# First stage of a two-layer DiT kernel: squares summed by TensorE in four pairs, first projection pair in halves of k, sine chains moved

## The chip, the cores and the metric

The kernel runs on one core of a Trainium2 chip. The metric is the device time of one execution in microseconds; lower is better. The engines are named as in the profile: PE (matmul), PEld (its weight load), DVE (VectorE), ACT (ScalarE), POOL (GpSimd), SP (the engine that issues the DMAs). PE has two clock levels, 1.2 and 2.4 GHz; a granted clock of 0.50 is the lower, 1.00 the upper.

## The reference, cut to what matters

Two layers on 512 latent and 256 context tokens, width 1024. What the change touches is the start of layer 0: the modulation vectors, the first RMS norm, the first columns of the projection `w_in`, and the small sine network that makes the convolution filters.

```python
sh1, sc1, ... = ada_mod(c, ada_w[0], ada_b[0])          # silu(c) @ w + b, in six chunks
csh1, csc1, ... = ada_mod(c_ctx, ada_w[0], ada_b[0])
h_lat = rmsnorm(x_lat, norm_mix[0]) * (1 + sc1) + sh1    # x * rsqrt(mean(x*x) + eps) * gain
h_ctx = rmsnorm(x_ctx, norm_mix[0]) * (1 + csc1) + csh1
u = h @ w_in                                             # x0, x1, v of the hyena half, q, k, v of the mLSTM half
u = dwconv(u[:, :1536], hy_conv_w) + hy_conv_b; g = v * x1
# filters: sin of a linear map, twice, then a linear map times a decay
h = sin(freq * (z @ fw1 + fb1)); h = sin(freq * (h @ fw2 + fb2)); h = (h @ fw3) * (decay + shift)
```

## The kernel before

The two token sets are laid side by side: a tile of x is 128 features x 768 tokens (512 + 256, the list `ALL`), and there are eight of them (k = 0 to 7). A product in f32 is made of three matmuls, high by high, high by low and low by high part, all on line 128 (`gemm`); for one k and one output block these are six matmuls, since each is made once for the 512 tokens and once for the 256. The high part of a weight block (`wh`) is cast by ACT on line 99 and the low part (`wl` = `raw` - `wh`) made by DVE on line 100. A "pair" below is two output blocks of 128 columns, one of v and one of x1 of the hyena half, which are made together.

The work of the stage, in the order of the source (lines 473 to 525): eight squares on ACT (lines 204 and 207) that DVE adds up in seven adds (line 208); six matmuls with a column of ones that sum over the features (line 214); the reciprocal square root on small DVE operations; six matmuls that spread it over 128 partitions (line 225), copied by ACT (line 481). `ada_pe` makes one chunk of the modulation vectors: eight matmuls of raw rows (line 278; a record pair for each), a copy by ACT (line 281), four matmuls with two columns (line 284) and the addition of the bias on DVE (line 93, `mod`). `sin_layer` is called twice: a matmul of 64 rows (line 373), six DVE operations on 64x768 (lines 377 to 382) and the sine on ACT (line 385), the second from the output of the first. Then, for every k: the scaled tile (`t`, line 96, DVE), the high part of h (line 522, ACT), its low part (line 96, DVE), and twelve matmuls of the first pair. `mod` has chunk 0 (shift, first half of k) and chunk 2 (scale, first half) ahead of k = 0, chunks 3 and 1 (the second half) ahead of k = 4. Behind the first pair come the convolution of its output (`conv`, three operations for each of 512 and 256 tokens: one on ACT, line 536, two on DVE, line 96), the filters (line 400, exponentials on line 402, sums and differences on lines 424 to 427) and the second pair.

The framework has a scheduler: the source gives each operation a priority, and the order on each engine is what the scheduler makes of it and of the tiles that are free. PSUM is split into three buffers `m`, two `g` and one `a`; there are five large temporaries `t`, four `u`, and two each of `raw`, `wh` and `wl`. Each engine runs its own queue strictly in that order, so a waiting instruction holds up all that stand behind it on its engine.

Of the kernel before, what the change touches and what calls it, by code (L numbers as in the profile page):

```python
# [12 lines left out]
ALU = mybir.AluOpType  # L13
# [4 lines left out]
P = 128  # L18
# [32 lines left out]
def hybrid_kernel(ctx: ExitStack, tc: tile.TileContext, A, out):  # L51
# [34 lines left out]
    def atile():  # L86
        return pa.tile([P, 512], F32, tag="a", name=nm("a"))
# [122 lines left out]
    def norm_scale(acc, n, dim, mid=None):  # L210
        nt = n // P
        ps = mtile()
        for i in range(nt):
            pe.matmul(ps[:, i:i + 1], acc[:, i * P:(i + 1) * P], ones[:, 0:1], start=True, stop=True)
        ms = sp.tile([P, 6], F32, tag="n1", name=nm("ms"))[:, :nt]
        y = sp.tile([P, 6], F32, tag="n2", name=nm("y"))[:, :nt]
        t = sp.tile([P, 6], F32, tag="n3", name=nm("nt"))[:, :nt]
        dve.tensor_scalar(ms, ps[:, :nt], 1.0 / (dim * RS * RS), EPS / (RS * RS), op0=ALU.mult, op1=ALU.add)
        rsqrt(y, ms, t)
        if mid:  # L220
            mid()
        g = [mtile() for _ in range((nt + 3) // 4)]
        for i in range(nt):
            o = g[i // 4][:, i % 4 * P:(i % 4 + 1) * P]
            pe.matmul(o, y[:, i:i + 1].to_broadcast([P, P]), ident, start=True, stop=True)
        return g
# [46 lines left out]
    def ada_pe(layer, ch):  # L273
# [7 lines left out]
        act.copy(ys, y)  # L281
        ps = atile()
# [87 lines left out]
    def sin_layer(w, kdim, b, rows=1):  # L370
        g = gtile()
        for z, (lo, n) in zip(hs_z, ALL):
            pe.matmul(g[:64, lo:lo + n], w, z[:kdim, :], start=True, stop=True)
        a = temp2()[:64]
        k = temp2()[:64]
        fb, fq = vec(b)[:64, :], vec("hy_freq")[:64, :]
        dve.tensor_scalar(a, g[:64, :T], fb, fq, op0=ALU.add, op1=ALU.mult)
# [97 lines left out]
    acc = temp()  # L475
    for k in range(KD):
        norm_acc(acc, x[k], k == 0)
    gp = norm_scale(acc, T, D)
# [3 lines left out]
    ada_pe(0, 2)  # L482
    w_first = [load_wk(A["w_in"][8], KD)]
# [26 lines left out]
    mod_half(0)  # L510
    for k in range(KD):
        if k == 3:
            ada_pe(0, 3)
            ada_pe(0, 1)
            mod_half(1)
        t = slot(4 + k, [P, 2, T], F32R)
        h.append((t[:, 0, :], t[:, 1, :]))
        f = temp()
        for c, (lo, n) in enumerate(ALL):
            s = slice(lo, lo + n)  # L520
            stt(f[:, s], x[k][:, s], a[:, k, c:c + 1], gsb0[:, s], ALU.mult, ALU.mult)
            act.activation(h[k][0][:, s], f[:, s], AF.Identity, bias=b[:, k, c:c + 1])
            stt(h[k][1][:, s], f[:, s], b[:, k, c:c + 1], f32(h[k][0][:, s]), ALU.add, ALU.subtract)
        for ps, w in ((first_v, w_first[0]), (first_x, w_first[1])):
            gemm(ps, w, h, ALL, ks=[k], first=k == 0, last=k == KD - 1)
    filter_fold()
# [979 lines left out]
```

## Time and profile before

| | us |
|---|---|
| runs shown | 1771.18, 1772.79, 1776.69 |
| median of them | 1772.79 |
| profiled execution | 1769.59 |
| its span, first to last instruction | 1767.8 |
| PE busy in the span | 1687.9 (95%) |
| first product of the first pair starts | 47.77 |
| last product of the first pair ends | about 75.3 |

PE is the engine that sets the end nearly everywhere; the stage that is changed lies in the first 78 us, where it isn't. The mean granted clock of the span is 0.987. In the trace the clock stands at 0.50 until 27.19 us (the records begin there), at 1.00 until 37.43, at 0.50 until 51.08, and then at 1.00 until 221.7. Times in the rows are us from the span's start; a matmul in f32 leaves two records.

### The profile page before, as it was taken

The numbers are of one execution on the slowest core, as the hardware profiler recorded it, in microseconds if no ns is written. First come the engines' busy times: TensorE is split into PE (matmuls) and PEld (weight loads), VectorE is DVE, ScalarE is ACT, GpSimd is POOL, SyncE is SP. The second block draws the span as 40 slices with busy tenths as digits, with TensorE's granted clock in tenths as the row PEclk, the third lists the DMA queues.
The fourth block names the chain that finished last, engine by engine and source line by source line (L and its number), as shares of the span: only waits on it lengthen the run. The fifth ranks groups of instructions, "written<-read, shape, count | busy, mean of one in ns | idle before, by whom it ended". The sixth has DMA issues, their size and how long they took to land.

```text
span 1767.8 us, 24375 instructions
## 1 busy us (share of the span) xinstructions
PE 1687.9 (95%) x9657; PEld 1435.2 (81%) x9657; DVE 1082.8 (61%) x1843; ACT 642.4 (36%) x1089; POOL 162.7 (9%) x165
## 2 busy tenths in 40 slices
PE   3989989998899999999999999989999999999997
PEld 2668777887888888888888888978888888888886
DVE  5786767749967456764355446487884644444445
ACT  3434232346543321132311334455553432232233
POOL 0141233005113000000000000000000300000001
PEclk9999989999999999999999999999999999999998
DMA  9026546412523134543255223110022223323322
GB/s 340 12 85 242 191 149 214 136 66 72 179 84 108 60 108 131 179 156 98 82 166 170 70 63 115 38 34 28 26 100 72 72 96 95 96 95 95 95 85 84
DMA packets 65748, 193.85 MB, mean 110 GB/s; under 512 B 7102, under 2 KB 17152, under 8 KB 65634
## 3 DMA queue, kind: packets, MB, share of 16 engines
q1 hardware_dynamic: 65634, 192.29, 33.4%
q8 instruction: 76, 1.25, 0.3%
q14 instruction: 38, 0.31, 0.1%
HBM read 178.64 MB, written 13.63 MB: 109 GB/s over the span
## 4 chain that ended last, share of the span: by engine, by line
PE 60%; issue 22%; DVE 7%; ACT 2%; POOL 1%; POOLq 0%; DVEq 0%; ACTq 0%
PE g L128 47%; PE g L1245 2%; DVE s L96 1%; DVE t L93 1%; PE m L1263 1%; PE m L104 1%; PE m L105 1%; PE m L103 1%; PE m L128 1%; DVE s L100 1%; PE g L103 1%; PE g L104 1%; PE g L105 1%; PE a L104 1%; PE a L103 1%
## 5 line engine op out<-in xcount | busy, mean ns | idle before, releaser
L128 PE MATMUL g<-s,wh 128*128 128x512 f32 (+1 forms) x4440 | 1067.2, 349 | 3.6 <-ACT u L1254 1.4
L128 PEld LDWEIGHTS g<-s,wh 128*128 128x128 f32 x4440 | 721.5, 189 | 124.6 <-issue 5.2
L128 PE MATMUL g<-s,wl 128*128 128x512 f32 (+2 forms) x2220 | 650.2, 348 | 1.9 <-DVE wl L100 1.9
L99 ACT CAST wh<-raw 128x1024 fp32r<-128x1024 f32 (+4 forms) x217 | 210.9, 972 | 646.5 <-PE g L128 556.4
L128 PEld LDWEIGHTS g<-s,wl 128*128 128x128 f32 x2220 | 365.5, 188 | 59.9 <-DVE wl L100 3.4
L100 DVE TENSOR_TENSOR wl<-raw,wh 128x1024 fp32r<-128x1024 f32 (+4 forms) x217 | 248.0, 1144 | 226.0 <-ACT wh L99 221.2
L96 DVE SCALAR_TENSOR_TENSOR acc<-ada,sc,acc 128x512 f32<-128x512 f32 x224 | 162.6, 763 | 27.7 <-DMA ada<-in_ada_dram 26.1
L96 DVE SCALAR_TENSOR_TENSOR s<-g,mod,s 128x512 f32<-128x512 f32 (+1 forms) x104 | 63.0, 625 | 146.0 <-PE g L128 145.2
L96 DVE SCALAR_TENSOR_TENSOR t<-g,vecs,t 128x511 f32<-128x511 f32 x200 | 128.5, 643 | 27.8 <-ACT t L536 22.8
L93 DVE TENSOR_TENSOR t<-t,g 128x768 f32<-128x768 f32 (+2 forms) x52 | 41.3, 794 | 109.2 <-PE g L128 109.1
L536 ACT ACTIVATE t<-g,vecs 128x512 f32<-128x512 f32 x84 | 58.5, 696 | 87.7 <-DVE t L96 62.4
L1245 PE MATMUL g<-s,s 128*128 128x512 f32 (+1 forms) x320 | 64.7, 344 | 3.7 <-DVE s L93 2.6
L1245 PEld LDWEIGHTS g<-s,s 128*128 128x128 f32 x320 | 48.8, 188 | 10.8 <-DVE s L93 4.1
L1078 ACT ACTIVATE t<-t 128x768 f32<-128x768 f32 (+1 forms) x42 | 31.0, 739 | 68.8 <-DVE t L96 68.8
L250 POOL TENSOR_SCALAR t<-t,A,mod 128x256 f32<-128x256 f32 x20 | 21.5, 1074 | 373.7 <-DVE t L93 364.5
L100 DVE TENSOR_TENSOR s<-m,s 128x512 fp32r<-128x512 f32 (+1 forms) x90 | 50.3, 590 | 6.9 <-ACT s L99 6.6
L99 ACT CAST s<-m 128x512 fp32r<-128x512 f32 (+1 forms) x90 | 42.5, 514 | 32.3 <-PE m L1263 24.2
L207 ACT ACTIVATE t<-s 128x256 f32<-128x256 f32 (+2 forms) x60 | 31.9, 549 | 29.7 <-DVE s L96 24.5
L1345 POOL TENSOR_TENSOR s<-s,t 128x256 f32<-128x256 f32 x8 | 5.5, 725 | 361.9 <-ACT t L1341 361.9
L1254 ACT ACTIVATE u<-g,mx 128x768 f32<-128x768 f32 x32 | 28.9, 905 | 25.0 <-DVE mx L1252 25.0
L1188 POOL MEMSET s<- 64x768 f32 x1 | 0.7, 734 | 398.6 <-PE g L128 398.6
L100 DVE TENSOR_TENSOR s<-t,s 128x768 fp32r<-128x768 f32 (+1 forms) x44 | 36.0, 818 | 0.0
(357 smaller groups left out, 1824.2 us busy)
## 6 DMA issues: line engine op xcount, KB each, us to landing
raw<-in_up_dram SPq DMA_DIRECT2D x88, 512.0 KB, 3.5
ada<-in_ada_dram SPq DMA_DIRECT2D x82, 512.0 KB, 3.5
raw<-in_down_dram SPq DMA_DIRECT2D x32, 512.0 KB, 3.6
raw<-in_w_in_dram SPq DMA_DIRECT2D x24, 512.0 KB, 3.7
raw<-in_w_out_dram SPq DMA_DIRECT2D x16, 512.0 KB, 3.4
s<-in_ada_dram SPq DMA_DIRECT2D x14, 512.0 KB, 10.2
s<-in_xT_dram SPq DMA_DIRECT2D x8, 768.0 KB, 4.9
raw<-in_down_dram SPq DMA_DIRECT2D x16, 384.0 KB, 3.1
```

Of the source, the lines that this page charges most:

```text
L93: return dve.tensor_tensor(o, a, b, op=op)
L96: return dve.scalar_tensor_tensor(o, a, s, b, op0=op0, op1=op1)
L99: act.copy(h, src)
L100: eng.tensor_tensor(l, src, f32(h), op=ALU.subtract)
L103: pe.matmul(o, s[0], m[0], start=start, stop=False)
L104: pe.matmul(o, s[0], m[1], start=False, stop=False)
L105: pe.matmul(o, s[1], m[0], start=False, stop=stop)
L128: pe.matmul(ps[r][:, :n] if type(ps) is list else ps[:, lo:lo + n], w[a][:, k - k0, :], mv[k][b][:, lo:lo + n], start=first and k == ks[0] ...
L207: act.activation(sq, xa, AF.Square)
L536: act.activation(d, s, AF.Identity, scale=w[:, 1:2], bias=bias)
L1078: act.activation(t[:, :n], t[:, :n], AF.Silu, **({} if f else dict(bias=zs)))
L1245: pe.matmul(g[:, lo:lo + w_], s_, m_[:, lo:lo + w_], start=n == 0, stop=n == 4)
```

## The change

- `norm_scale` takes a tuple of partial sums. The squares are added in four pairs (four DVE adds, not seven), PE sums each pair (24 matmuls with the ones column, not 6), and one small DVE reduction adds the four.
- The first sine layer (argument, fold, sine) stands ahead of the norm. The argument's matmul of the second layer stands behind the copies of the norm; its fold and its sine stand behind the last chunk of the first pair.
- `ada_pe` is cut in `ada_rows` (matmuls of rows and the copy) and `ada_cols` (the rest). The rows of chunk 2 are issued while DVE makes the reciprocal root (`mid`).
- The loop over k is cut in `first_scaled`, `first_h` and `first_gemm` and written out; chunk k = 3 of the pair is issued in two halves around the columns of the last modulation chunk.

```diff
+        accs = acc if type(acc) is tuple else (acc,)
+        for c, v in enumerate(accs):
+            for i in range(nt):
+                o = c * nt + i
+                pe.matmul(ps[:, o:o + 1], v[:, i * P:(i + 1) * P], ones[:, 0:1], start=True, stop=True)
...
+        if len(accs) > 1:
+            sums = ms
+            dve.tensor_reduce(ms, ps[:, :len(accs) * nt].rearrange("p (c i) -> p i c", i=nt), axis=AX.X, op=ALU.add)
...
+    def sin_arg(w, kdim, b):
+        a = temp2()[:64]
+        fb, fq = vec(b)[:64, :], vec("hy_freq")[:64, :]
         for z, (lo, n) in zip(hs_z, ALL):
-            pe.matmul(g[:64, lo:lo + n], w, z[:kdim, :], start=True, stop=True)
+            g = mtile()
+            pe.matmul(g[:64, :n], w, z[:kdim, :], start=True, stop=True)
+            dve.tensor_scalar(a[:, lo:lo + n], g[:64, :n], fb, fq, op0=ALU.add, op1=ALU.mult)
+        return a
...
-    acc = temp()
-    for k in range(KD):
-        norm_acc(acc, x[k], k == 0)
-    gp = norm_scale(acc, T, D)
+    sin_1 = sin_arg(hs_w3[:33, 1024:1088], 33, "hy_fb1")
+    sin_fold(sin_1)
+    acc = []
+    for k in range(0, KD, 2):
+        acc.append(temp())
+        norm_acc(acc[-1], x[k], True)
+        norm_acc(acc[-1], x[k + 1], False)
+    acc = tuple(acc)
+    w_first = []
+
+    def mod_rows():
+        w_first.append(ada_rows(2))
+
+    gp = norm_scale(acc, T, D, mod_rows)
...
-    ada_pe(0, 2)
-    w_first = [load_wk(A["w_in"][8], KD)]
+    ada_cols(0, 2, w_first.pop())
+    sin_out(sin_1)
+    sin_2 = sin_arg(hs_w3[:64, 1088:1152], 64, "hy_fb2")
+    w_first.append(load_wk(A["w_in"][8], KD))
...
-    ada_pe(0, 0)
-    sin_layer(hs_w3[:33, 1024:1088], 33, "hy_fb1")
-    sin_layer(hs_w3[:64, 1088:1152], 64, "hy_fb2", 2)
...
+    mod_half(0)
+    for k in range(3):
+        first_scaled(k)
+    ada_cols(0, 0, ada_rows(0))
+    first_h(0)
+    first_gemm(0)
+    first_scaled(3)
+    first_h(1)
+    first_gemm(1)
+    r3 = ada_rows(3)
+    for k in (2, 3):
+        first_h(k)
+    first_gemm(2)
+    ada_cols(0, 3, r3)
+    mod_half(1)
+    r1 = ada_rows(1)
+    first_gemm(3, slice(0, 1))
+    for k in range(4, 7):
+        first_scaled(k)
+    ada_cols(0, 1, r1)
+    first_gemm(3, slice(1, 2))
+    first_h(4)
+    first_gemm(4)
+    first_scaled(7)
+    for k in range(5, KD):
+        first_h(k)
+        first_gemm(k)
+    sin_fold(sin_2)
+    sin_out(sin_2, 2)
```

How the instructions then stand, at three places. First PE at the start of the first pair. `m_352` takes the rows of modulation chunk 3, `g_252` the argument of the second sine layer, `acc_88` and `acc_89` hold the output of the first; `g_289` is the v block of the first pair, `s_292` h of k = 0. Before:

```order
L278 MATMUL m_352<-s_267,s_90 32x512
L278 MATMUL m_352<-s_268,s_90 32x512
L278 MATMUL m_352<-s_269,s_90 32x512
L373 MATMUL g_252<-acc_88,s_90 64x512
L373 MATMUL g_252<-acc_89,s_90 64x256
L128 MATMUL g_289<-s_292,wh_208 128x512
L128 MATMUL g_289<-s_292,wh_208 128x256
```

After; here `m_241` takes the second part of that argument (the first stands four rows ahead of it), `m_294` the rows of chunk 0, `a_229` and `a_305` the columns of chunks 2 and 0, and `g_282` and `s_311` are the block and h:

```order
L385 MATMUL m_241<-acc_89,s_90 64x256
L294 MATMUL a_229<-comb,u_216 128x2 x4
L285 MATMUL m_294<-s_106,s_90 32x512
L285 MATMUL m_294<-s_107,s_90 32x512
L285 MATMUL m_294<-s_106,s_90 32x512
L285 MATMUL m_294<-s_107,s_90 32x512
L285 MATMUL m_294<-s_108,s_90 32x512
L285 MATMUL m_294<-s_109,s_90 32x512
L285 MATMUL m_294<-s_108,s_90 32x512
L285 MATMUL m_294<-s_109,s_90 32x512
L294 MATMUL a_305<-comb,u_303 128x2 x4
L128 MATMUL g_282<-s_311,wh_246 128x512
```

The argument of the second sine layer moved from between the modulation rows and the first product to eleven rows ahead of the first product.

Second DVE behind the first pair. `wl_559` (before) and `wl_579` (after) are the low part of the v block of the second pair; `ada_503`, `ada_504` and `ada_523`, `ada_524` the convolved output of the first pair; `t_`, `u_` with an `m_` behind the arrow are filter halves. Before:

```order
L96 SCALAR_TENSOR_TENSOR t_529<-u_526,m_523 128x512
L96 SCALAR_TENSOR_TENSOR u_538<-u_536,m_532 128x512
L100 TENSOR_TENSOR wl_559<-raw_556,wh_558 128x1024
L96 SCALAR_TENSOR_TENSOR ada_503<-g_289,vecs,ada_503 128x511
L96 SCALAR_TENSOR_TENSOR ada_504<-g_290,vecs,ada_504 128x511
L96 SCALAR_TENSOR_TENSOR ada_503<-g_289,vecs,ada_503 128x511
L96 SCALAR_TENSOR_TENSOR ada_504<-g_290,vecs,ada_504 128x511
L96 SCALAR_TENSOR_TENSOR ada_503<-g_289,vecs,ada_503 128x255
L96 SCALAR_TENSOR_TENSOR u_539<-u_536,m_533 128x512
```

After:

```order
L96 SCALAR_TENSOR_TENSOR ada_523<-g_282,vecs,ada_523 128x255
L96 SCALAR_TENSOR_TENSOR ada_524<-g_283,vecs,ada_524 128x255
L96 SCALAR_TENSOR_TENSOR u_558<-u_556,m_552 128x512
L96 SCALAR_TENSOR_TENSOR u_559<-u_556,m_553 128x512
L439 TENSOR_TENSOR u_562<-t_548,u_558 128x512
L441 TENSOR_TENSOR u_563<-t_549,u_559 128x512
L440 TENSOR_TENSOR t_548<-t_548,u_558 128x512
L442 TENSOR_TENSOR t_549<-t_549,u_559 128x512
L93 TENSOR_TENSOR s_511<-u_562,s_510 128x512
L93 TENSOR_TENSOR s_515<-t_548,s_514 128x512
L93 TENSOR_TENSOR s_517<-u_563,s_516 128x512
L100 TENSOR_TENSOR wl_579<-raw_576,wh_578 128x1024
```

The low part moved from ahead of the convolution to behind the convolution, the filter halves, their sums and differences and three of their low parts.

Third PE at the start of the second pair, whose v block is `m_568`, `m_569` before. Before:

```order
L128 MATMUL g_290<-s_467,wl_219 128x512
L128 MATMUL g_290<-s_467,wl_219 128x256
L400 MATMUL m_533<-s_90,acc_88 128x512
L128 MATMUL m_568<-s_292,wh_558 128x512
L128 MATMUL m_569<-s_292,wh_558 128x256
L128 MATMUL m_568<-s_292,wh_558 128x512
L128 MATMUL m_569<-s_292,wh_558 128x256
L128 MATMUL m_568<-s_292,wl_559 128x512
L128 MATMUL m_569<-s_292,wl_559 128x256
```

After, where it is `m_588`, `m_589`, and `g_590` is its x1 block:

```order
L415 MATMUL m_552<-s_90,acc_88 128x512
L415 MATMUL m_553<-s_90,acc_88 128x512
L128 MATMUL m_588<-s_311,wh_578 128x512 x2
L128 MATMUL g_590<-s_311,wh_584 128x512
L128 MATMUL g_590<-s_311,wh_584 128x256
L128 MATMUL g_590<-s_311,wh_584 128x512
L128 MATMUL g_590<-s_311,wh_584 128x256
L128 MATMUL m_589<-s_311,wh_578 128x256 x2
L415 MATMUL m_706<-s_90,acc_88 128x512
L128 MATMUL m_588<-s_311,wl_579 128x512
L128 MATMUL m_589<-s_311,wl_579 128x256
L128 MATMUL m_588<-s_331,wh_578 128x512
```

The first matmul with the low part, `wl_579`, now has eight matmuls with high parts and five filter matmuls (three of them shown) between it and the first pair; all that use h of k = 1 and later stand behind it.

## Rows read from the trace of the kernel before

**Rows 1.** The page's head: the span, and busy time of each engine.

```profile
span 1767.8 us, 24375 instructions
PE 1687.9 (95%) x9657; PEld 1435.2 (81%) x9657; DVE 1082.8 (61%) x1843; ACT 642.4 (36%) x1089; POOL 162.7 (9%) x165
```

**Rows 2.** Windows: start:end, us, busy of each engine (records), clock, DMA share, GB/s.

```profile
27.20:37.40 10.20, 6.53 (x50) 2.79 (x42) 7.49 (x15) 2.75 (x5) 0.00 (x0) 1.00 1.03 397
47.77:51.10 3.33, 3.33 (x11) 2.85 (x11) 3.15 (x5) 0.00 (x0) 0.00 (x0) 0.50 0.00 0
51.10:66.31 15.21, 14.55 (x85) 9.04 (x83) 6.18 (x14) 7.70 (x13) 0.00 (x0) 1.00 0.00 0
66.31:75.36 9.05, 9.05 (x50) 7.39 (x49) 6.86 (x15) 3.71 (x7) 0.00 (x0) 1.00 0.01 3
```

**Rows 3.** Timeline of PE, first stage: start, us, line, out<-in, count, [idle before <-releaser].

```profile
17.40 2.72 PE L214 MATMUL m<-ones,t 128*128 128x1 f32 x12 [10.31 <-DVE t L208]
...
24.84 3.07 PE L278 MATMUL m<-s,s 128*32 128x512 f32 x16
...
29.64 1.94 PE L278 MATMUL m<-s,s 128*32 128x512 f32 x16
...
45.02 2.82 PE L373 MATMUL g<-acc,s 64*64 64x512 f32 x4 [9.78 <-ACT acc L385]
47.77 1.65 PE L128 MATMUL g<-s,wh 128*128 128x512 f32 x4
...
64.40 1.98 PE L400 MATMUL m<-s,acc 64*128 64x512 f32 x6
66.31 1.53 PE L128 MATMUL g<-s,wh 128*128 128x512 f32 x5
```

**Rows 4.** Timeline of ACT and POOL: sines, table load, last squares, filter fold.

```profile
13.93 1.58 ACT L207 ACTIVATE t<-s 128x768 f32<-128x768 f32 x2 [0.41 <-DMA s<-in_xT_dram]
44.34 0.94 ACT L385 ACTIVATE acc<-u 64x512 f32<-64x512 f32 x2 [2.47 <-DVE u L382]
61.87 1.28 ACT L402 ACT_TABLE_LOAD   x1
```

```profile
40.00 3.56 POOL L390 TENSOR_TENSOR s<-s 64x512 f32<-64x512 f32 x2 [39.55 <-DMA s<-in_fw_dram]
```

**Rows 5.** Timeline of DVE, first stage and the hand-over to the second pair.

```profile
15.33 2.01 DVE L208 TENSOR_TENSOR t<-t,t 128x768 f32<-128x768 f32 x2
...
32.02 3.65 DVE L96 SCALAR_TENSOR_TENSOR t<-s,A,t 128x256 f32<-128x256 f32 x7
35.59 1.06 DVE L377 TENSOR_SCALAR u<-g,vecs 64x768 f32<-64x768 f32 x1
36.58 0.15 DVE L93 TENSOR_TENSOR mod<-a,vecs 128x8 f32<-128x8 f32 x1
...
42.36 1.48 DVE L96 SCALAR_TENSOR_TENSOR s<-t,mod,s 128x256 fp32r<-128x256 f32 x1
...
75.08 1.22 DVE L100 TENSOR_TENSOR wl<-raw,wh 128x1024 fp32r<-128x1024 f32 x1 [2.19 <-ACT wh L99]
```

**Rows 6.** Timeline of PE at the hand-over.

```profile
75.30 1.12 PE L400 MATMUL m<-s,acc 64*128 64x512 f32 x2
76.35 0.97 PE L128 MATMUL m<-s,wh 128*128 128x512 f32 x4
77.16 0.51 PE L128 MATMUL m<-s,wl 128*128 128x512 f32 x2
```

**Rows 7.** Groups of DVE instructions, 66 to 92 us: xcount, busy us, mean ns, idle before.

```profile
L96 DVE SCALAR_TENSOR_TENSOR ada<-g,vecs,ada 128x511 f32<-128x511 f32 x4 | 2.7, 740 | 0.0
L96 DVE SCALAR_TENSOR_TENSOR ada<-g,vecs,ada 128x255 f32<-128x255 f32 x4 | 1.8, 479 | 0.0
L96 DVE SCALAR_TENSOR_TENSOR t<-u,m 128x512 f32<-128x512 f32 x3 | 2.0, 670 | 0.0
L424 DVE TENSOR_TENSOR u<-t,u 128x512 f32<-128x512 f32 x1 | 0.7, 683 | 0.0
L93 DVE TENSOR_TENSOR s<-u,s 128x512 fp32r<-128x512 f32 x2 | 1.4, 690 | 0.0
```

More of the change, by code (lines that the diff above doesn't have):

```diff
@@ L212, in norm_scale @@
         ps = mtile()
-        for i in range(nt):
-            pe.matmul(ps[:, i:i + 1], acc[:, i * P:(i + 1) * P], ones[:, 0:1], start=True, stop=True)
+        accs = acc if type(acc) is tuple else (acc,)
[3 more added lines that the diff above has]
+                pe.matmul(ps[:, o:o + 1], v[:, i * P:(i + 1) * P], ones[:, 0:1], start=True, stop=True)
         ms = sp.tile([P, 6], F32, tag="n1", name=nm("ms"))[:, :nt]
@@ L217, in norm_scale @@
         t = sp.tile([P, 6], F32, tag="n3", name=nm("nt"))[:, :nt]
-        dve.tensor_scalar(ms, ps[:, :nt], 1.0 / (dim * RS * RS), EPS / (RS * RS), op0=ALU.mult, op1=ALU.add)
+        sums = ps[:, :nt]
+        if len(accs) > 1:
+            sums = ms
+            dve.tensor_reduce(ms, ps[:, :len(accs) * nt].rearrange("p (c i) -> p i c", i=nt), axis=AX.X, op=ALU.add)
+        dve.tensor_scalar(ms, sums, 1.0 / (dim * RS * RS), EPS / (RS * RS), op0=ALU.mult, op1=ALU.add)
         rsqrt(y, ms, t)
@@ L271, in hybrid_kernel, with ada_rows @@
     dve.tensor_reduce(comb, ident.rearrange("p (u c) -> p c u", c=32)[:, 0:2, :], axis=AX.X, op=ALU.add)
-    def ada_pe(layer, ch):
+    def ada_rows(ch):
         y = mtile()
@@ L281, in ada_pe, with ada_cols @@
         act.copy(ys, y)
+        return ys
+    def ada_cols(layer, ch, ys):
         ps = atile()
@@ L368, in hybrid_kernel, with sin_fold @@
     kd = dp.tile([6, P, 1536], F32, name="kd")
-    def sin_layer(w, kdim, b, rows=1):
-        g = gtile()
+    def sin_arg(w, kdim, b):
+        a = temp2()[:64]
+        fb, fq = vec(b)[:64, :], vec("hy_freq")[:64, :]
         for z, (lo, n) in zip(hs_z, ALL):
-            pe.matmul(g[:64, lo:lo + n], w, z[:kdim, :], start=True, stop=True)
-        a = temp2()[:64]
+            g = mtile()
+            pe.matmul(g[:64, :n], w, z[:kdim, :], start=True, stop=True)
+            dve.tensor_scalar(a[:, lo:lo + n], g[:64, :n], fb, fq, op0=ALU.add, op1=ALU.mult)
+        return a
+    def sin_fold(a):
         k = temp2()[:64]
-        fb, fq = vec(b)[:64, :], vec("hy_freq")[:64, :]
-        dve.tensor_scalar(a, g[:64, :T], fb, fq, op0=ALU.add, op1=ALU.mult)
         dve.tensor_scalar(k, a, 1.0 / (2.0 * math.pi), MAGIC, op0=ALU.mult, op1=ALU.add)
@@ L382, in sin_layer, with sin_out @@
         dve.tensor_scalar(a, a, 3.1415925, -3.1415925, op0=ALU.min, op1=ALU.max)
+    def sin_out(a, rows=1):
         for z, (lo, n) in zip(hs_z, ALL):
@@ L509, in hybrid_kernel, with first_scaled, first_h, first_gemm @@
     first_v, first_x = gtile(), gtile()
[L510 to L515, printed above, removed]
+    fs = {}
+    def first_scaled(k):
+        fs[k] = temp()
+        for c, (lo, n) in enumerate(ALL):
+            s = slice(lo, lo + n)
+            stt(fs[k][:, s], x[k][:, s], a[:, k, c:c + 1], gsb0[:, s], ALU.mult, ALU.mult)
+    def first_h(k):
+        f = fs.pop(k)
         t = slot(4 + k, [P, 2, T], F32R)
         h.append((t[:, 0, :], t[:, 1, :]))
-        f = temp()
         for c, (lo, n) in enumerate(ALL):
             s = slice(lo, lo + n)
-            stt(f[:, s], x[k][:, s], a[:, k, c:c + 1], gsb0[:, s], ALU.mult, ALU.mult)
             act.activation(h[k][0][:, s], f[:, s], AF.Identity, bias=b[:, k, c:c + 1])
             stt(h[k][1][:, s], f[:, s], b[:, k, c:c + 1], f32(h[k][0][:, s]), ALU.add, ALU.subtract)
-        for ps, w in ((first_v, w_first[0]), (first_x, w_first[1])):
+    def first_gemm(k, part=slice(0, 2)):
+        for ps, w in ((first_v, w_first[0]), (first_x, w_first[1]))[part]:
             gemm(ps, w, h, ALL, ks=[k], first=k == 0, last=k == KD - 1)
+    mod_half(0)
[27 more added lines that the diff above has]
+    sin_out(sin_2, 2)
     filter_fold()
```

## The prediction

> **What bounds the kernel now.** I read the page's head first: PE is busy for 1687.9 of 1767.8 us [rows 1], so over the kernel time is PE's work, and only a stretch in which PE waits, or runs at the lower clock, can give something back. Then the windows and PE's timeline of the first 78 us. The longest wait of PE inside the stage stands ahead of the second sine argument: 9.78 us idle, ended by ACT's sine at 45.02; the argument itself takes 2.82 more, and the first product starts at 47.77 [rows 3]. It starts at the lower clock, which stays until about 51.1 [rows 2]. From 66.31 on PE is busy without a gap (9.05 of 9.05 [rows 2]) to the end of the first pair, which I put at 75.36. So what the stage is worth is where that end falls. Last I read who hands over to the second pair, since a gain counts only if PE can go on: before, PE does one filter matmul and four high-part matmuls and then finds the low part `wl` just made (75.08 + 1.22 = 76.30; the first matmul with it at 77.16 [rows 5, 6]). The hand-over costs 77.16 - 75.36 = 1.8 us, part of it useful work.
>
> **The change part by part: the first stage.** *Sums.* DVE drops three adds, but the last add waits for the last squares as before: they end at 13.93 + 1.58 = 15.5 [rows 4], the last add at 15.33 + 2.01 = 17.34 [rows 5]. The order puts the first sine (0.94 for two [rows 4]) ahead of the last pair's squares on ACT, so that add can come up to 0.9 later; the first three sums lie beside the loading of x, and the last six matmuls cost the 2.72 that all sums cost before [rows 3]. Plus a reduction like the small ones (0.15 to 0.17 [rows 5]): between -1 and +1 us for the norm's end; I take 0, since DVE's queue behind it, below, is what sets the first product.
>
> *Modulation rows and scaled tiles.* Rows 2 move into the wait for the reciprocal root, rows 0 follow. Chunk 0's shift was finished on DVE at 36.58, behind seven scaled tiles (3.65) and the sine's 1.06 at 35.59 [rows 5]. The scaled tiles still stand ahead of it, the 1.06 does not: 36.58 - 1.06 = 35.5, then 0.17 and one 512 wide ACT operation, which I put at 0.7 (a 768 wide square takes 1.58/2 = 0.8 [rows 4]): first product T0 = 36.4 if the clock is raised in time, 11.4 us earlier than 47.77. If PE is still at the lower clock through both groups of rows, each costs 3.07 instead of 1.94 [rows 3], 1.1 more, twice, and the sine argument that now stands ahead of the columns costs up to its 2.82, of which 1.8 remains after overlap by my estimate: T0 = 36.4 + 2.2 + 1.8 = 40.4.
>
> *From the first product to chunk k = 4.* Before this took 66.31 - 47.77 = 18.5 us. PE's work in it, in us at full clock, is 3.33/2 + 14.55 - 1.98 (filter matmuls that now stand behind the pair) = 14.2 [rows 2, 3]; all at the lower clock it is 28.4. Before, the sine wait had let DVE make nearly all scaled tiles and low parts of k = 0 to 3 ahead; now PE starts beside them, and POOL's fold of the filter weights (3.56 us at 40.00 [rows 4]) lies under it, under which a 256 wide low part took 1.48 [rows 5] where its like takes about 0.5. So I take neither end but 22.5 us, 4 more than before, between 14.2 and 28.4. The rest of the pair is k = 4 to 7 and stays 9.05 [rows 2]. End of the pair E: 36.4 + 22.5 + 9.05 = 68.0 with the early clock, 40.4 + 31.55 = 72.0 with the late one. Gain of the stage g = 75.36 - E: 7.4 or 3.4.
>
> *Second sine.* It costs ACT and DVE what it did, and two more table loads at 1.28 each [rows 4]; they lie in ACT's idle time behind the last h, and PE needs the sine for the filters only. I cost it at nothing, because the hand-over below is later; without that cover it would be 1.28.
>
> **The change part by part: the hand-over.** This is the term that decides. In the order of before `wl` of the second pair stands on DVE ahead of the convolution; after, it stands behind all of this, which can begin only at E, because the convolution reads the finished pair and the filters need the matmuls that stand behind the pair on PE: about 1.0 for the first filter matmul (two records 1.12 [rows 6]); four 511 wide operations, 2.7; four 255 wide, 1.8; four filter halves at 0.67, 2.7; four sums and differences at 0.68, 2.7; three low parts at 0.69, 2.1; `wl`, 1.2 [rows 5, 7]. That is 14.2; the rows run into each other by some 0.08 each (four 0.74 in a row took less than their sum), 15 times, 1.2: 13.0 us from E to `wl`. PE has the filter matmuls and eight high-part matmuls to do and then stands; everything of k = 1 and later is queued behind the first `wl` matmul, and since PE runs without gaps from there, the whole rest of the program waits with it. Against that: the 1.8 that the hand-over cost before; and 1.6 of work that PE does in the wait and needn't do later (one filter matmul 0.9, four x1 high-part matmuls 0.7 [rows 6]). And PE idles for about 10 us, as long as the 9.78 us after which the clock stayed low from 45.02 to 51.1 [rows 2, 3], which cost 6.1/2 = 3.0; bounds 0 and 3.0, I take 2.4, because part of the wait is filled with matmuls.
>
> The hand-over loses 13.0 - 1.8 - 1.6 + 2.4 = 12.0 us. **Sum:** 12.0 - g: +4.6 with the early clock, +8.6 with the late one. The stage breaks even only if the pair ends 12.0 us earlier, at 63.4. I see nothing later that gives the loss back: the order is the same there apart from names.
>
> **The base.** The profiled execution took 1769.59, 1.8 outside its span, and is 3.2 below the median, 1772.79. I take the mean of 1769.59, 1771.18 and 1772.79, 1771.2. What a measurement can tell from no change is 0.3%, 5.3 us.
>
> **The rivals.** *Late clock (forecast).* The clock was low until 27.19, and the sums at 17.40 did not raise it: sixteen records of rows at 24.84 took 3.07, the next sixteen 1.94 [rows 3]. If the many thin sums count as little, T0 is late: 1771.2 + 8.6 = 1779.8.
>
> *Early clock.* There are four times as many sums, spread over the 10.31 us that PE waited ahead of 17.40 [rows 3], so PE is no longer idle ahead of the norm. The trace has no stretch like it: E = 68.0, 1771.2 + 4.6 = 1775.8. The Trainium skill, "TensorE: Matmul & The Clock Gate", section "Part 1: The HAM clock gate (the "warmup" mystery)", has the throttled state as the default, which activity of PE lifts: by that sentence this case is the likelier one and the sum 1775.8, by the row at 17.40 the late one. The row is of this kernel, so I go by it, with a smaller lead.
>
> *Full clock and no waits (the other side).* PE goes from T0 = 36.4 at the upper clock, DVE keeps ahead of it, and the stretch to k = 4 is its bare 14.2: E = 59.7, g = 15.7, -3.7, and if the clock then doesn't fall in the hand-over, another -2.4: 1765.1 to 1767.5. It turns to a gain from E = 63.4. Against it: DVE must make four h tiles in that time, under POOL, and the second group of modulation rows has a copy and columns in a chain ahead of k = 4.
>
> *Low clock throughout the stage.* 40.4 + 28.4 + 9.05 gives E = 77.9, +14.5: 1785.7. For it: before, the clock fell at 37.4 and rose only at 51.1 [rows 2].
>
> *The wait isn't there.* If DVE's order on the chip were another, g would stay whole: 1763.8 to 1767.8. The order of each engine's queue is fixed, so I give this no more than a small share of the third rival's chance.
>
> **How the numbers follow.** Late clock 0.45, early clock 0.30, full clock or no wait 0.15, low throughout 0.10. Slower by over 0.3%: most of the first (0.38), a third of the second (0.10), all of the last but little (0.09): 0.57. Faster by over 0.3%: under two thirds of the third (0.09) and 0.02 from run to run: 0.11. Within: 0.32. The likeliest case gives 1779.8, so 1780; the range goes from 1770 (the early case less the 5 us that T0 and the stretch may be off) to 1787 (the low clock and a little over).
>
> **What would show it.** PE's first product at 36 to 41 instead of 47.77, with no wait for a sine ahead of it; k = 4 starting at 58 to 63; the pair ending at 67 to 72; then a wait of PE for `wl`, put down to DVE, of about 10 us, with DVE busy without a gap from the convolution on; `wl` 13 us after the pair's end; a stretch of low clock behind it. Wrong would be the prediction if the pair ended before 63, or if PE's wait for `wl` were under 5 us.

## The result and the profile after

The changed kernel takes 1784.43 us (median of four runs, 1782.83 to 1787.23), the kernel before 1774.32 (1771.18 to 1776.69): 1.0062 times as long, 95% interval 1.0044 to 1.0080, some 10 us. It is slower by more than the 0.3% that can be told from no change, and inside the range. It is 4.4 us above the predicted 1780; 3.1 of them are the base, since the kernel before took 1774.32 here and not the 1771.2 that the prediction started from. The profiled execution of after is the slowest of its four (1787.23), that of before (1769.59) is below all four of its kernel, so the two spans differ by 17.6 us; what happens up to some 150 us can be compared instruction by instruction, the whole spans can't.

The head of the page of after, which answers to [rows 1]:

```profile
span 1785.4 us, 24446 instructions
PE 1714.6 (96%) x9693; PEld 1452.0 (81%) x9693; DVE 1084.4 (61%) x1843; ACT 645.5 (36%) x1091; POOL 159.2 (9%) x165
```

PE's timeline of after (start, us, line, out<-in, count, idle before and what ended it), which answers to [rows 3] and [rows 6]:

```profile
10.96 7.99 PE L217 MATMUL m<-ones,t 128*128 128x1 f32 x36 [3.66 <-DVE t L208]
18.88 1.91 PE L285 MATMUL m<-s,s 128*32 128x512 f32 x2
20.73 2.72 PE L217 MATMUL m<-ones,t 128*128 128x1 f32 x12
23.38 3.62 PE L285 MATMUL m<-s,s 128*32 128x512 f32 x6
...
27.57 1.05 PE L285 MATMUL m<-s,s 128*32 128x512 f32 x2
...
34.49 1.94 PE L285 MATMUL m<-s,s 128*32 128x512 f32 x16
...
41.73 1.73 PE L128 MATMUL g<-s,wh 128*128 128x512 f32 x2 [3.47 <-ACT s L548]
...
64.72 2.71 PE L128 MATMUL g<-s,wh 128*128 128x512 f32 x7 [1.01 <-ACT s L548]
...
74.79 3.03 PE L415 MATMUL m<-s,acc 64*128 64x512 f32 x8
80.01 0.70 PE L128 MATMUL m<-s,wh 128*128 128x512 f32 x2 [2.19 <-ACT ada L594]
81.19 1.34 PE L128 MATMUL g<-s,wh 128*128 128x512 f32 x4 [0.47 <-DVE ada L96]
...
82.88 2.07 PE L415 MATMUL m<-s,acc 64*128 64x512 f32 x2
90.44 1.00 PE L128 MATMUL m<-s,wl 128*128 128x512 f32 x2 [5.49 <-DVE wl L100]
```

The first product starts at 41.73, 6.0 us earlier than before, with no wait for a sine. Yet k = 4 starts only 1.6 earlier (64.72 against 66.31), and the pair ends at 74.86, 0.5 earlier than 75.36. The first matmul with the low part of the second pair follows at 90.44, 15.6 us later, where it took 1.8 before. PE works for 7.4 of the 15.6 and stands for 8.2, in three pieces (2.19, 0.47 and 5.49 us); the last ends with the low part. Why is seen on DVE, which works through its queue almost without a gap; its timeline of after, which answers to [rows 5] and [rows 7]:

```profile
75.95 0.69 DVE L96 SCALAR_TENSOR_TENSOR t<-u,m 128x512 f32<-128x512 f32 x1 [4.30 <-PE m L415]
76.56 2.72 DVE L96 SCALAR_TENSOR_TENSOR ada<-g,vecs,ada 128x511 f32<-128x511 f32 x4
...
79.78 1.65 DVE L96 SCALAR_TENSOR_TENSOR ada<-g,vecs,ada 128x255 f32<-128x255 f32 x4
81.34 1.28 DVE L96 SCALAR_TENSOR_TENSOR u<-u,m 128x512 f32<-128x512 f32 x2
82.54 1.52 DVE L439 TENSOR_TENSOR u<-t,u 128x512 f32<-128x512 f32 x1
83.98 1.21 DVE L441 TENSOR_TENSOR u<-t,u 128x512 f32<-128x512 f32 x1
...
89.18 1.21 DVE L100 TENSOR_TENSOR wl<-raw,wh 128x1024 fp32r<-128x1024 f32 x1
```

Two windows of after (start:end, us, busy of PE, PEld, DVE, ACT, POOL with records, clock, DMA share, GB/s): the wait, and what PE then does at the lower clock.

```profile
74.85:90.44 15.59, 7.43 (x19) 3.06 (x18) 14.49 (x21) 8.85 (x13) 5.73 (x5) 0.71 0.22 68
90.44:95.17 4.73, 4.73 (x15) 4.05 (x16) 1.69 (x2) 0.00 (x0) 0.00 (x0) 0.50 0.69 211
```

How much of that stays is read from one instruction that is the same in both programs, the tenth low part of a weight block on DVE, some 50 us on: before it starts at 138.48,

```profile
138.48 1.22 DVE L100 TENSOR_TENSOR wl<-raw,wh 128x1024 fp32r<-128x1024 f32 x1 [2.41 <-ACT wh L99]
```

and after at 150.85, 12.4 us later:

```profile
150.85 1.23 DVE L100 TENSOR_TENSOR wl<-raw,wh 128x1024 fp32r<-128x1024 f32 x1 [3.97 <-ACT wh L99]
```

The other 5.2 of the 17.6 come later. The granted clock falls more often there in this execution (after has 0.50 at 289.7 to 296.6 and 443.3 to 446.7, where before has 1.00), but that this is the whole of it isn't shown. In the trace of the first edit below, which as a kernel is no slower than before, the same lag grows by 4.1 us (from -0.5 at this instruction to 3.6 at the end of the span), so most of the 5.2 seems to belong to the one execution of before that was profiled.

### The profile page after: what moved, and what is told of

It is laid out like the page before. It is cut to its first block, busy times and chain, and to the rows that moved or that the text cites. A ratio compares the mean times of both kernels' runs of the same rounds, so it can differ in the third digit from the quotient of the medians.

```text
span 1785.4 us, 24446 instructions
## 1 busy us (share of the span) xinstructions
PE 1714.6 (96%) x9693; PEld 1452.0 (81%) x9693; DVE 1084.4 (61%) x1843; ACT 645.5 (36%) x1091; POOL 159.2 (9%) x165
## 4 chain that ended last, share of the span: by engine, by line
PE 60%; issue 21%; DVE 6%; ACT 2%; POOL 1%; POOLq 0%; DVEq 0%; ACTq 0%
PE g L128 46%; PE g L1303 2%; DVE t L93 1%; PE m L1321 1%; PE m L104 1%; PE m L105 1%; PE m L103 1%; DVE s L96 1%; PE m L128 1%; PE g L103 1%; DVE s L100 1%; PE g L104 1%; PE g L105 1%; PE a L103 1%; PE a L104 1%
## 5 line engine op out<-in xcount | busy, mean ns | idle before, releaser
L96 DVE SCALAR_TENSOR_TENSOR acc<-ada,sc,acc 128x512 f32<-128x512 f32 x224 | 162.8, 764 | 26.6 <-DMA ada<-in_ada_dram 24.9
L207 ACT ACTIVATE t<-s 128x256 f32<-128x256 f32 (+2 forms) x57 | 29.6, 534 | 28.8 <-DVE s L96 24.5
L128 PE MATMUL m<-s,wh 128*128 128x512 f32 (+1 forms) x120 | 34.5, 382 | 2.2 <-ACT ada L594 2.2
```

Source lines behind the costliest of these rows:

```text
L96: return dve.scalar_tensor_tensor(o, a, s, b, op0=op0, op1=op1)
L128: pe.matmul(ps[r][:, :n] if type(ps) is list else ps[:, lo:lo + n], w[a][:, k - k0, :], mv[k][b][:, lo:lo + n], start=first and k == ks[0] ...
L207: act.activation(sq, xa, AF.Square)
```

## The experiments

Each was timed beside the kernel before on the same chip; the ratio is to that kernel, with its 95% interval. "Pair's end", "first product" and "first low-part matmul" are read from PE's timeline of the run.

| edit | median us (before) | ratio | first product | pair's end | first low-part matmul |
|---|---|---|---|---|---|
| before | | 1 | 47.77 | 75.36 | 77.16 |
| the change | 1784.43 (1774.32) | 1.0062 | 41.73 | 74.86 | 90.44 |
| low part first | 1772.71 (1773.82) | 0.9989 | 41.47 | 74.67 | 78.23 |
| DVE sums | 1778.15 (1773.82) | 1.0033 | 37.21 | 68.59 | 84.18 |
| both | 1767.15 (1773.82) | 0.9964 | 37.27 | 68.70 | 72.26 |
| before, sine 1 alone | 1771.45 (1773.82) | 0.9993 | 38.69 | 72.49 | 77.94 |
| before, PE sums alone | 1775.71 (1771.46) | 1.0020 | 49.23 | 76.82 | 78.62 |
| POOL's product small | 1780.81 (1771.46) | 1.0047 | 41.84 | 75.05 | 88.22 |
| second sine back | 1777.22 (1771.46) | 1.0025 | 42.84 | 75.56 | 80.88 |
| rows behind the norm | 1780.88 (1775.28) | 1.0038 | 38.91 | 72.71 | 88.29 |
| both, shift early | 1767.81 (1771.46) | 0.9979 | 36.67 | 71.33 | 76.55 |
| both, again | 1767.85 (1775.28) | 0.9964 | 37.23 | 68.50 | 72.07 |
| both, rows behind the norm | 1764.71 (1773.45) | 0.9953 | 36.90 | 69.63 | 73.19 |

Differences in us between two runs are those of their medians, each less its own kernel before. Where the ratios give another figure that matters, it stands beside.

**Low part first.** The hand-over alone is mended in the changed kernel.

```diff
+    second = [load_wk(win[n + 1], KD) for n in (8, 4)]
     for j in range(4):
...
-            wv, wx = [load_wk(win[n + j], KD) for n in (8, 4)]
+            wv, wx = second if j == 1 else [load_wk(win[n + j], KD) for n in (8, 4)]
```

> The changed kernel, with the loads and the split of the second pair's weights written ahead of the first pair's convolution, so that DVE makes the low part before it begins the convolution; the first stage is as in the changed kernel. Theory (the loss is the hand-over): the first product stays at about 41.7 us and the pair's end at about 75; the first matmul with the low part comes 2 to 4 us after the pair's end instead of 15.6 (74.8 to 90.4), and the stretch of low clock behind it goes. That is 11 to 13 us less than the changed kernel: about 1773, the same as before within 0.3%. Rival (the loss is the first stage, that is the sums and the clock, and the wait of PE for the low part is covered by other work): no less than 1782, since the first stage isn't touched.

Measured: 1772.71, ratio 0.9989 (0.9978 to 1.0000). Against their own kernels before, the change stands at +10.1 and this at -1.1: 11.2 us, all of the loss (12.9 by the ratios). PE's timeline of this kernel at the hand-over:

```profile
74.60 3.02 PE L415 MATMUL m<-s,acc 64*128 64x512 f32 x8
77.55 0.73 PE L128 MATMUL m<-s,wh 128*128 128x512 f32 x2
78.23 0.50 PE L128 MATMUL m<-s,wl 128*128 128x512 f32 x1
```

The pair ends as in the changed kernel, the wait is gone, and the clock stays at 1.00 from 67.85 to 221.45. The theory holds: with the first stage as it is in the changed kernel, mending the hand-over takes the whole loss away. It doesn't say that the first stage has nothing to give; that is the next edit's question.

**DVE sums.** The sums alone are put back.

```diff
-    acc = []
-    for k in range(0, KD, 2):
-        acc.append(temp())
-        norm_acc(acc[-1], x[k], True)
-        norm_acc(acc[-1], x[k + 1], False)
-    acc = tuple(acc)
+    acc = temp()
+    for k in range(KD):
+        norm_acc(acc, x[k], k == 0)
```

> The changed kernel with one part undone: squares added on DVE (seven adds) and summed by six matmuls, as before the change. Theory: the norm's sums end at about 20.3 us instead of 23.45, the first product starts some 3 us earlier than 41.7, and the pair ends 2 to 4 us earlier than 74.8; the hand-over still costs 15 us. Time 1781, 3 less than the changed kernel. Rival (the sums on PE are the loss): back to 1774. Second rival (the sums are hidden behind the loading of x, and the clock follows them): no change or up to 3 us more than the changed kernel, because with fewer matmuls the clock is raised later.

Measured: 1778.15, ratio 1.0033 (1.0021 to 1.0045): +4.3 against +10.1, so 5.8 us less than the changed kernel where 3 were expected. The start of this kernel on PE:

```profile
18.57 2.72 PE L217 MATMUL m<-ones,t 128*128 128x1 f32 x12 [11.37 <-DVE t L208]
21.22 3.63 PE L285 MATMUL m<-s,s 128*32 128x512 f32 x10
24.77 0.49 PE L232 MATMUL m<-cst,y 128*128 128x128 f32 x2
...
37.21 1.73 PE L128 MATMUL g<-s,wh 128*128 128x512 f32 x2 [2.89 <-ACT s L545]
```

The sums end at 21.3 instead of 23.45, the first product starts 4.5 earlier, and the pair ends 6.3 earlier. The hand-over still takes 15.6 (68.59 to 84.18). So the fewer sums on PE are better by about twice what was expected; the rival that the clock would be raised later without the many sums is wrong: it rises at 24.8 here and at 26.9 in the changed kernel.

**Both.** The two edits above together.

> Both edits together: the low part of the second pair ahead of the convolution, and the sums as before the change. Theory: the two add up, 11 to 13 us and 3 us less than the changed kernel, so 1770, some 4 us less than before (0.2%). Rival (the hand-over hides the sums): the same as with the first edit alone, 1773.

Measured: 1767.15, ratio 0.9964 (0.9951 to 0.9978), 6.7 less than before. From the change this is 16.8; the single edits give 11.2 + 5.8 = 17.0. The two add up: with the hand-over mended, 6.0 us at the pair's end (74.67 to 68.70) are 5.6 at the end of the program.

**Before, sine 1 alone.** One part of the change in the kernel before.

```diff
+    sin_layer(hs_w3[:33, 1024:1088], 33, "hy_fb1")
     acc = temp()
...
     ada_pe(0, 0)
-    sin_layer(hs_w3[:33, 1024:1088], 33, "hy_fb1")
```

> The kernel before, with one part of the change alone: the first sine layer (argument, fold, sine) ahead of the norm, the second where it was. Theory (a wait taken from the stage is worth only what the pair's end moves): the 9.78 us wait of PE for the sine goes and the first product starts at 38 to 40 us instead of 47.77, but the pair's end comes only 2 to 4 us earlier than 75.3, because PE now meets the second modulation group and DVE's low parts; and the hand-over is between as short as before (1.8) and 4 us longer. Time 1770 to 1776. Rival (the wait is worth what it lasts): 9.78 and the low clock behind it, 10 to 12 us less: 1763.

Measured: 1771.45, ratio 0.9993 (0.9983 to 1.0003), no change. PE's timeline:

```profile
38.69 1.14 PE L128 MATMUL g<-s,wh 128*128 128x512 f32 x4 [1.95 <-ACT s L522]
...
77.27 0.87 PE L128 MATMUL m<-s,wh 128*128 128x512 f32 x2 [2.87 <-DVE t L96]
77.94 0.63 PE L128 MATMUL m<-s,wl 128*128 128x512 f32 x1
```

The wait of 9.78 us is gone and the first product is 9.1 earlier. The pair's end is 2.9 earlier, and then PE waits 2.87 for DVE's first filter half, which holds an `m` buffer that the second pair needs: its first low-part matmul is at 77.94, 0.8 later than before. The longest wait of the stage is taken away, and that alone is worth nothing.

**Before, PE sums alone.** The kernel before with the four pair sums (the reverse of the DVE sums' diff, and the new `norm_scale`).

> The kernel before, with the sums of the changed kernel alone: four pairs of squares added on DVE, each summed by PE. Theory (the thin sums cost the norm's end time, but before the change the sine wait is later than the norm): the last group of sums still takes 2.72 us behind the last pair, and no modulation rows stand ahead of it, so the norm ends within 1 us of before; the first product still waits for the sine, at 47 to 49 us; 1774, within 0.2% of before. Rival (the sums on PE are bad by themselves): 3 us slower, 1777, with the first product at 50 or later.

Measured: 1775.71, ratio 1.0020 (1.0009 to 1.0031). PE's timeline shows 48 records in a row:

```profile
10.95 10.40 PE L217 MATMUL m<-ones,t 128*128 128x1 f32 x48 [3.59 <-DVE t L208]
```

The sums end at 21.35, 1.2 later than before (20.12), the first product at 49.23 and the pair's end at 76.82 are 1.5 later. The theory said hidden within 0.2%, and the ratio lies just there, but it isn't hidden: the delay arrives at the pair's end. The rest of the 3.5 us (by the ratio; 4.2 by the medians) comes behind it, at the x1 block of the second pair, where before PE had no wait:

```profile
91.27 1.01 PE L128 MATMUL g<-s,wl 128*128 128x512 f32 x2 [3.00 <-DVE wl L100]
```

DVE was late with that low part because its sums ran beside POOL's product and took up to 2.35 (line 433 at 83.73), where before they kept 0.69; on this, see the last section. So the ratio isn't the price of the sums alone. Neither expectation is clearly right; the sign is the rival's.

**POOL's product small.** In the changed kernel all but 8 of 768 columns of POOL's product of the first pair, and its folding, are left out.

```diff
+        if j == 0:
+            (pool if j < 3 else dve).tensor_tensor(gs[0][:, 0, 0:8], vt[:, 0:8], xt[:, 760:768], op=ALU.mult)
+        else:
+            (pool if j < 3 else dve).tensor_tensor(vt, vt, xt, op=ALU.mult)
...
-        for lo, n in ALL:
+        for lo, n in ALL if j else ():
```

> The changed kernel, with nearly all of POOL's product and folding of the first pair left out (8 columns are made of 768, so the result lacks that block). Theory (the wait for the low part is 15.6 us and not 13 because DVE's sums run beside POOL): the sums and differences take 0.69 each again instead of 0.94 to 1.52, the low part comes 12.7 to 13.3 us after the pair's end, and the time is 2 to 3 us less than the changed kernel, 1781 to 1782. Rival (DVE is slow there for another reason, as the waiting on ACT's casts): the wait stays 15 to 16 us, 1784.

Measured: 1780.81, ratio 1.0047 (1.0031 to 1.0062), against 1.0062: 0.15%, 2.7 us; by the medians only 0.8, and the two intervals overlap, so the times alone don't show it. The traces do: the tenth low part on DVE starts at 148.22, where the change has 150.85, 2.6 us earlier. DVE's timeline of this kernel:

```profile
82.73 0.69 DVE L439 TENSOR_TENSOR u<-t,u 128x512 f32<-128x512 f32 x1
83.33 0.69 DVE L441 TENSOR_TENSOR u<-t,u 128x512 f32<-128x512 f32 x1
...
86.94 1.22 DVE L100 TENSOR_TENSOR wl<-raw,wh 128x1024 fp32r<-128x1024 f32 x1
```

The sums take 0.69 again, not 1.52 and 1.21, and the first low-part matmul comes 13.2 after the pair's end (75.05 to 88.22). What was missing in the predicted 13.0 is what POOL does to DVE's sums.

**Second sine back.** The fold and the sine of the second layer stand ahead of the first pair's low parts again.

```diff
     ada_cols(0, 0, ada_rows(0))
+    sin_fold(sin_2)
+    sin_out(sin_2, 2)
     first_h(0)
...
-    sin_fold(sin_2)
-    sin_out(sin_2, 2)
     filter_fold()
```

> The changed kernel with one part undone: fold and sine of the second layer ahead of the first pair's low parts again, not behind its last chunk. The scheduler then puts the low part of the second pair ahead of the convolution by itself, and makes the first four filter matmuls no later than the pair's end. Theory (moving the second sine is what pushed the low part back): the first product comes about 1 us later than 41.7, the pair's end 0 to 2 us later than 74.8, the first matmul with the low part 4 to 6 us behind it instead of 15.6; 8 us less than the changed kernel, 1776. Rival (the halves of the first pair or the norm's order did it): the wait stays over 10 us and the time over 1782.

Measured: 1777.22, ratio 1.0025 (1.0013 to 1.0037): 0.37%, 6.6 us less than the change (4.4 by the medians; 6.9 at the tenth low part, 143.91). The first low-part matmul comes 5.3 after the pair's end. DVE's timeline, where the low part now stands ahead of the convolution with no edit there:

```profile
75.29 1.22 DVE L100 TENSOR_TENSOR wl<-raw,wh 128x1024 fp32r<-128x1024 f32 x1 [2.80 <-ACT wh L99]
76.43 3.17 DVE L96 SCALAR_TENSOR_TENSOR ada<-g,vecs,ada 128x511 f32<-128x511 f32 x5
```

So it is the move of the second sine that made the scheduler put the low part behind the convolution; the halves of the first pair and the norm's order, which stay here, don't do it alone.

**Rows behind the norm.** Another part of the change undone.

```diff
-    def mod_rows():
-        w_first.append(ada_rows(2))
-
-    gp = norm_scale(acc, T, D, mod_rows)
+    gp = norm_scale(acc, T, D)
+    w_first.append(ada_rows(2))
```

> The changed kernel with one part undone: the rows of modulation chunk 2 stand behind the norm again, not in the wait for the reciprocal root, so that no rows stand ahead of the last group of sums. Theory (the sums are late on PE because 36 records of sums at the low clock end at 18.95, over 1 us behind the last add, and a rows matmul of 1.91 stands between them and the last group): the sums end at 21.6 us instead of 23.45, but the rows come behind the spreading of the norm and the columns of chunk 2 no earlier, so the first product stays at 41 to 43 us and the time within 2 us of the changed kernel: 1783 to 1786. Rival (the norm's end alone sets the first product): 1.9 us earlier throughout, 1782 or less.

Measured: 1780.88, ratio 1.0038 (1.0025 to 1.0052), +5.6 against +10.1: 4.5 us less than the change, with intervals that overlap. PE's timeline:

```profile
10.74 10.55 PE L217 MATMUL m<-ones,t 128*128 128x1 f32 x48 [3.69 <-DVE t L208]
23.38 2.93 PE L232 MATMUL m<-cst,y 128*128 128x128 f32 x12 [2.09 <-DVE y L96]
26.24 3.08 PE L285 MATMUL m<-s,s 128*32 128x512 f32 x16
...
38.91 1.73 PE L128 MATMUL g<-s,wh 128*128 128x512 f32 x2 [3.33 <-ACT s L546]
```

The first product is 2.8 earlier, where the theory had it stay, and the pair's end and the first low-part matmul 2.2: the rival is right, and 2.2 us is what the trace shows; the rest of the 4.5 isn't seen there. The sums end at 21.29, as they do in the kernel with DVE sums. The spreading of the norm (line 232) is done at 26.3, where in the change it is interleaved with rows until 29.7. Putting work in a wait of 2.09 us delayed what the wait was for.

**Both, shift early.** To the two edits, a third: the scale of k = 1 to 3 is made with a column of ones that is computed from the first shift, so that their scaled tiles stand behind the shift on DVE.

```diff
...
-    mod_half(0)
-    for k in range(3):
-        first_scaled(k)
+    mod_part(0, 1, 1.0)
+    first_scaled(0)
     ada_cols(0, 0, ada_rows(0))
...
+    dve.tensor_scalar(one, mods[0][:, 0, 0:1], 0.0, 1.0, op0=ALU.mult, op1=ALU.add)
+    mod_part(1, 4, one)
...
```

`mod_part(lo, hi, unit)` makes the scale of k = lo to hi - 1, with `unit` in the place of the 1 in (1 + scale).

> The two edits of the fastest kernel so far, and a third: the scaled tiles of k = 1 to 3 are made to wait for the first modulation shift (their scale is computed with a column of ones that is made from it), so that DVE makes the shift's bias addition right behind the first scaled tile. Theory (the first product waits for DVE's queue): first product at 35.3 to 36 us instead of 37.27, PE's wait ahead of it 1 us instead of 2.9, the clock perhaps without its fall at 35; the pair's end 1 to 3 us earlier than 68.3: 1765 to 1766. Rival (the order behind the pair decides more than the start): the scheduler now puts the second low part behind filter halves and the x1 block waits, so that the gain goes there: 1767 to 1770.

Measured: 1767.81, ratio 0.9979 (0.9970 to 0.9988). The first product is at 36.67, only 0.6 earlier: PE then waited 0.43 for ACT's cast of the weights. The clock rose at 27.2, and the pair ended at 71.33, 2.6 later than without the edit. From there to the first low-part matmul it took 5.2 and not 3.6, with a wait of PE of 1.71 ahead of the filter matmuls at 73.04, for which the profile shows no releaser. The gain isn't there; the rival had the time, and its reason covers at most these 1.7: the larger part of the loss lies ahead of the pair's end. **Both, again** asked whether the earlier clock of that kernel was luck:

> The kernel with the low part ahead of the convolution and the sums as before the change, once more, beside the one with the early shift on the same chip. Theory: 0.36% less than before again, 0.9964, the pair's end near 68. Rival (its pair's end at 68.3 was a lucky clock, which rose at 24.9 there and at 27.2 with the early shift): 0.998, like the other.

Measured: 1767.85, ratio 0.9964 again, pair's end at 68.50, clock raised at 24.5. It wasn't luck. Why the clock rose later with the early shift stays open.

**Both, rows behind the norm.** The version that the experiments pointed to: low part first, DVE sums, rows behind the norm.

> The fastest kernel so far (low part ahead of the convolution, sums as before the change), and the rows of modulation chunk 2 behind the norm again. Theory (rows put ahead of the spreading of the norm delay it on PE, at the low clock): the spreading starts at 23.2 us instead of 24.8, the columns of chunk 2 follow no later than 28.3, the first product comes 0 to 1.5 us earlier than 37.2, the pair's end 0 to 2 us earlier than 68.3: ratio to before 0.995 to 0.9965. Rival (the rows now run at the low clock behind the spreading and the clock rises later than at 24.5): first product at 38 to 39 us, pair's end at 70 to 71, ratio 0.9975 to 0.9985, like the kernel with the early shift.

Measured: 1764.71, ratio 0.9953 (0.9939 to 0.9966), 8.7 us less than before and the fastest of all, though its interval overlaps that of the two edits alone. The first product is 0.3 earlier but the pair's end, 69.63, 1.1 later, since the clock rose at 26.6 and fell once more; so the time agrees with the theory and the pair's end lies between the two. That it beats the two edits alone isn't shown; that it beats the kernel before is. With the DVE sums, then, no difference is shown between rows in the wait and rows behind the norm.

## Why the prediction was right, step by step

It was right on the mechanism: the stage got shorter, and the hand-over, by DVE's new order, lost more than the stage gave. By its own signs it was less good. The low part behind the wait and the low clock came as described, and neither sign of being wrong did. But the first product (41.73), k = 4 (64.72) and the pair's end (74.86) all came later than their ranges, and PE stood for 8.2 us instead of about 10. That the total still came out near is in part luck, as the sum below shows.

**The hand-over** was the deciding term, and it is what the low-part edit shows: 11.2 us. Its size was 13.0 us from the pair's end to `wl`; it measured 15.6 to the first matmul with it. The train of DVE operations was sized right (13.2 without POOL); the step that failed is that the prices of the sums were taken from the kernel before, where they kept 0.68 to 0.69 beside POOL's product and it was the product that took longer (6.80). The low clock behind the wait was put at 2.4: PE ran from 90.44 to 95.17 at 0.50, 4.73/2 = 2.4. (The clock had fallen at 81.52 already, inside the wait.)

**The second sine** was costed at nothing, and on PE it is: ACT ends it in time for the filter matmuls at 74.79. But it was the move that changed DVE's order, as its undoing shows. The prediction read the order's result and didn't ask for its cause; the sum needed none.

**The sums** were the worst step: between -1 and +1, 0 taken. They ended at 23.45 instead of 20.12, 3.3 later, and putting them back is worth 5.8. The text took the first three groups as lying beside the loading of x. They do, but 36 records at the lower clock end at 18.95, 1.4 after the last add (DVE, after),

```profile
16.61 0.96 DVE L208 TENSOR_TENSOR t<-t,t 128x768 f32<-128x768 f32 x1 [1.36 <-ACT t L207]
```

and then a rows matmul of 1.91 stands ahead of the last group. Without those rows (rows behind the norm) the same sums end at 21.29, so 2.2 of the 3.3 hang on the two together. A queue that is covered still has to be empty in time.

**The first product**: 40.4 forecast for the late clock, 41.73 measured, for another reason; that the two are near is luck. The clock rose at 26.90, 0.3 earlier than before (27.19), and the second group of rows took 1.94, not 3.07. Of the 5.3 us over the early 36.4, 3.6 came from the norm, whose reciprocal root was done at 25.49 against 21.93. The last of its operations, after and then before:

```profile
25.32 0.17 DVE L96 SCALAR_TENSOR_TENSOR y<-nt,y 128x6 f32<-128x6 f32 x1
```

```profile
21.76 0.17 DVE L96 SCALAR_TENSOR_TENSOR y<-nt,y 128x6 f32<-128x6 f32 x1
```

The rest of the 5.3 isn't taken apart. **From there to k = 4**: 22.5 forecast, 64.72 - 41.73 = 23.0 measured. **The rest of the pair**: 9.05 forecast, 10.1 measured. PE had waited 1.01 us for h of k = 4, behind the second shift, and the clock stood at 0.50 from 64.45 to 67.86, a window of after:

```profile
64.45:67.86 3.41, 3.14 (x9) 2.66 (x10) 3.41 (x7) 3.41 (x8) 0.00 (x0) 0.50 0.02 5
```

So the gain of the stage was 0.5, where 3.4 was forecast.

**The sum** by its own form with these: 15.6 - 1.8 - 1.6 + 2.4 - 0.5 = 14.1 in the profiled execution; the matched low part says 12.4, the medians 10.1. So two terms of the forecast +8.6 were short, by 5.5 together: the stage's gain (2.9) and the train beside POOL (2.6). Against them stands what the prediction held to be nothing, something later that gives the loss back. Behind the second pair PE's filter matmuls still stand 13.5 later than before (94.63 before):

```profile
108.12 1.98 PE L415 MATMUL m<-s,acc 64*128 64x512 f32 x6
```

But then PE waits in the kernel before, for a low part and again 1.14 us for a filter half at 119.69,

```profile
107.23 0.62 PE L128 MATMUL g<-s,wl 128*128 128x512 f32 x2 [1.27 <-DVE wl L100]
```

and in the changed kernel, which comes later, it doesn't, but for 0.30 at 130.52. At the ninth low part on DVE (132.53 before, 143.35 after) the lag is down to 10.8; a stretch at 0.50 from 142.96 to 146.37, which before doesn't have, makes it 12.4. That the forecast difference came within 1.5 us of the medians is owed to this and to the spread between executions, and so to luck; 3.1 us more of the miss are the base.

**The rivals.** Late against early clock was put on the row of the kernel before, where the clock hadn't risen behind the sums. With four times as many it rose at 26.90 here and, in the kernel before with PE sums alone, at 28.64, against 27.19. So the extra sums didn't bring it forward, as the late rival had it; but its price, the rows at the lower clock, was paid in part only, and the first product was late by the norm. The Trainium skill, "TensorE: Matmul & The Clock Gate", section "Part 1: The HAM clock gate (the "warmup" mystery)", has activity of PE lifting the throttle; the prediction took that for the early clock, which would have given 1775.8. The trace shows no early rise: PE is busy for all of 10.96 to 26.90 (15.94 of 15.94 us), and the upper clock is recorded from 26.90 only (a lone rows matmul takes 1.91 at 18.88, and 1.05 at 27.57). Full clock without waits fell with g = 0.5; the rival that the wait isn't there fell with 90.44. The low clock throughout, 1785.7, lies nearest to the measured time, but it isn't what happened: the clock was at 1.00 from 26.90 to 40.56 and from 47.38 to 64.45.

## What to carry to other kernels

A wait that is taken from the front of a stage is worth what the stage's end moves and what the next stage can take up: here 9.8 us of waiting were worth 0.5 to 2.9 at the pair's end, and nothing where DVE stood in the way. After moving code under a scheduler, read each engine's new order at the hand-over to the next stage; one small-looking instruction (a low part) behind a train of others cost more than the stage could give. Work put into a wait isn't free if it stands ahead of what the wait is for: here it cost 2.2 us with the sums on PE, while with the sums on DVE no cost was shown.

## What the runs showed of the hardware that was not expected

The clock didn't rise during the thin sums. In the changed kernel 36 records with one column took 7.99 us without a pause, and the clock rose 8 us after them, at 26.90. In the kernel before it rose at 27.19 with 12 such records (2.72 us), and at 28.64 with 48 in a row (10.40 us). In all of these kernels it rose between 24.5 and 29.9 us, after the first matmuls of the modulation or of the norm's spreading had begun.

DVE's sums and POOL's product slow each other. A DVE sum of 128x512 takes 0.69 alone and 0.94 to 1.52 beside POOL's product and folding in after (up to 2.35 in other runs); POOL's product (128x768) took 1.82 in after, where it took 6.80 before, while DVE's sums beside it kept 0.69. POOL's timeline, after:

```profile
81.69 1.82 POOL L619 TENSOR_TENSOR ada<-ada,ada 128x768 f32<-128x768 f32 x1 [35.27 <-DVE ada L96]
```

and before:

```profile
82.03 6.80 POOL L561 TENSOR_TENSOR ada<-ada,ada 128x768 f32<-128x768 f32 x1 [38.47 <-ACT s L432]
```

The ends fit two engines that take turns in after: POOL's product ends at 83.51 and the first sum at 84.06, 0.55 later, and DVE's next four operations (three sums and a low part) each end 0.55 behind one of POOL's foldings, too. Before, POOL's product ends 1.7 behind a row of DVE's sums and low parts without a gap (to 87.12), as if it had got no turn until then. Which of the two yields isn't the same in all kernels, and no run here tells what decides it. The Trainium skill, "VectorE: DVE Perf Modes", section "⚠️ Two Vector instructions with no wait between them", has an instruction with two SBUF inputs read one of them through an interface that is shared with GpSimd. The trace agrees as far as it goes: the sums, with two SBUF inputs, are slow, and the filter halves, which read one input from PSUM, kept 0.68 (the second of the 1.28 at 81.34) with POOL already at work.
